# One input tile of a rotary-embedding kernel loaded on ScalarE's DMA ring instead of SyncE's

## The chip, the cores and the metric

One core of one Trainium2 chip. The profile's names for the engines are used: DVE is VectorE, ACT is ScalarE, POOL is GpSimd, PE is TensorE and SP is SyncE. SP and ACT issue the transfers here; the queue of transfers that one of them has issued is called its ring. A transfer moves as packets and has landed when its completion is signalled. The metric is the device time of one execution in microseconds (us), measured over several executions. The profile's span is about 1.8 us shorter than this time. Each timed kernel was run in rounds beside the kernel before on the same chip.

## The reference

```python
# x: 8 x 8 x 1024 x 64 float32; cos, sin: 1024 x 32 float32
x_first, x_second = x[..., :32], x[..., 32:]
out_first  = x_first * cos - x_second * sin
out_second = x_first * sin + x_second * cos
return concatenate([out_first, out_second], axis=-1)
```

x has 16.8 MB and so has the output. There are four multiplications and two additions for each pair of elements, so that most of the work is moving bytes.

## The kernel before

x is cut into 16 tiles of 128 partitions x 2048 elements (1.05 MB, 8 KB per partition). All 16 fit in SBUF at once and every tile has its own place, so no load waits for a buffer. The two tables come first, one on each ring; then all of x on SP's ring:

```python
nc.sync.dma_start(out=sn[0:Q], in_=sin_cached...)      # SP's ring
nc.scalar.dma_start(out=cs[0:Q], in_=cos_cached...)    # ACT's ring

xt = []
for first, n in [(0, 1), (1, 1)] + [(c, 2) for c in range(2, n_ch, 2)]:
    t = xp.tile([P, n, F], fp32, name=f"x{first}")
    nc.sync.dma_start(out=t, in_=xf[first:first + n]...)
    xt += [t[:, i] for i in range(n)]
```

The tables arrive on 32 partitions. DVE copies sine and ACT copies cosine into PSUM on all 128 partitions; POOL copies both within SBUF for its own tiles. Then the tiles are shared out:

```python
def vector_pool(c, cuts=(0, R)):      # DVE: products, POOL: sums, store on SP's ring
    s = tv.tile([P, F], fp32, name="vs")
    products(nc.vector, c, s, csp, snp)
    for n0, n1 in zip(cuts, cuts[1:]):
        sums(nc.gpsimd, c, s, n0, n1)
        store(nc.sync, c, n0, n1)
# vector_tensor(c): products on DVE, sums by TensorE, copied back by ACT, store on ACT's ring
# on_pool(c): all on POOL, store on SP's ring
def vector_alone(c):                  # all on DVE, store on ACT's ring
    products(nc.vector, c, acc, csp, snp)
    sums(nc.vector, c, acc, 0, R)
    store(nc.scalar, c)

vector_tensor(0)
on_pool(1)
vector_pool(2)
# ... (cut: 3 to 13)
vector_pool(14, (0, G, R))
vector_alone(15)
```

Tile 0 is DVE's first work on x. Tile 1, the one that the change moves, is POOL's first.

Of the kernel before, what the change touches and what calls it, by code (L numbers as in the profile page):

```python
# [1 line left out]

# [4 lines left out]


@with_exitstack
def kernel(  # L10
    ctx: ExitStack,
    tc: tile.TileContext,
    x: bass.AP,
    cos_cached: bass.AP,
    sin_cached: bass.AP,
    out: bass.AP,
):
    nc = tc.nc
    fp32 = mybir.dt.float32
    TT = mybir.AluOpType  # L20
    P = nc.NUM_PARTITIONS

    b, h, seq, hd = x.shape
    half = hd // 2
    R = 32
    F = R * hd
    T = R * half
    Q = seq // R
    reps = P // Q
    n_ch = (b * h * seq) // (R * P)  # L30
    G = 512 // half
    assert seq % R == 0 and P % Q == 0 and Q % 32 == 0

    xf = x.rearrange("b h s d -> (b h s d)").rearrange(
        "(c p m) -> c p m", p=P, m=F)
    of = out.rearrange("b h s d -> (b h s d)").rearrange(
        "(c p m) -> c p m", p=P, m=F)

    ctx.enter_context(tc.manual_schedule())
    const = ctx.enter_context(tc.tile_pool(name="const", bufs=1))  # L40
    xp = ctx.enter_context(tc.tile_pool(name="xp", bufs=1))
    tv = ctx.enter_context(tc.tile_pool(name="tv", bufs=6))
    tg = ctx.enter_context(tc.tile_pool(name="tg", bufs=1))
    pt = ctx.enter_context(
        tc.tile_pool(name="pt", bufs=1, space=bass.MemoryType.PSUM))
    pa = ctx.enter_context(
        tc.tile_pool(name="pa", bufs=1, space=bass.MemoryType.PSUM))

    cs = const.tile([P, T], fp32, name="cs")
    sn = const.tile([P, T], fp32, name="sn")  # L50
    plus = const.tile([P, P], fp32, name="plus")
    minus = const.tile([P, P], fp32, name="minus")
    csp = pt.tile([P, T], fp32, name="csp")
    snp = pt.tile([P, T], fp32, name="snp")
    acc = pa.tile([P, F], fp32, name="acc")


    nc.sync.dma_start(out=sn[0:Q], in_=sin_cached.rearrange("(p n) j -> p (n j)", p=Q))
    nc.scalar.dma_start(out=cs[0:Q], in_=cos_cached.rearrange("(p n) j -> p (n j)", p=Q))


    xt = []
    for first, n in [(0, 1), (1, 1)] + [(c, 2) for c in range(2, n_ch, 2)]:
        t = xp.tile([P, n, F], fp32, name=f"x{first}")
        nc.sync.dma_start(out=t, in_=xf[first:first + n].rearrange("c p m -> p c m"))
        xt += [t[:, i] for i in range(n)]

    nc.gpsimd.memset(plus, 0.0)
    nc.gpsimd.affine_select(out=plus, in_=plus, compare_op=TT.not_equal, fill=1.0,
                            base=0, pattern=[[-1, P]], channel_multiplier=1)  # L70
    nc.scalar.mul(minus, plus, -1.0)  # L71
    for r in range(reps):
        nc.vector.tensor_copy(out=snp[r * Q:(r + 1) * Q], in_=sn[0:Q])  # L73
        nc.scalar.copy(out=csp[r * Q:(r + 1) * Q], in_=cs[0:Q])  # L74
    for t in (sn, cs):
        for r in range(1, reps):
            nc.gpsimd.tensor_copy(out=t[r * Q:(r + 1) * Q], in_=t[0:Q])  # L77

    def rows(t, n0=0, n1=R):
        return t[:, n0 * hd:n1 * hd].rearrange("p (n k j) -> p n k j", k=2, j=half)  # L80

    def tab(t, n0=0, n1=R):
        v = t[:, n0 * half:n1 * half].rearrange("p (n o j) -> p n o j", o=1, j=half)
        return v.to_broadcast([P, n1 - n0, 2, half])

    def products(eng, c, s, ctab, stab):
        xr = rows(xt[c])
        eng.tensor_tensor(out=rows(s), in0=xr, in1=tab(stab), op=TT.mult)  # L88
        eng.tensor_tensor(out=xr, in0=xr, in1=tab(ctab), op=TT.mult)  # L89

    def sums(eng, c, s, n0, n1):
        xr, sr = rows(xt[c], n0, n1), rows(s, n0, n1)
        eng.tensor_tensor(out=xr[:, :, 0], in0=xr[:, :, 0], in1=sr[:, :, 1], op=TT.subtract)  # L93
        eng.tensor_tensor(out=xr[:, :, 1], in0=xr[:, :, 1], in1=sr[:, :, 0], op=TT.add)  # L94

    def store(q, c, n0=0, n1=R):
        q.dma_start(out=of[c][:, n0 * hd:n1 * hd], in_=xt[c][:, n0 * hd:n1 * hd])

    def on_pool(c):
        s = tg.tile([P, F], fp32, name="gs")  # L100
        products(nc.gpsimd, c, s, cs, sn)
        sums(nc.gpsimd, c, s, 0, R)
        store(nc.sync, c)

    def vector_pool(c, cuts=(0, R)):
# [6 lines that stand above are left out]
    def vector_tensor(c):  # L112
        s = tv.tile([P, F], fp32, name="vs")
        products(nc.vector, c, s, csp, snp)
        for n0 in range(0, R, G):
            xr, sr = rows(xt[c], n0, n0 + G), rows(s, n0, n0 + G)
            a = acc[:, n0 * hd:(n0 + G) * hd].rearrange("p (k n j) -> p k n j", k=2, j=half)
            for k in range(2):
                nc.tensor.matmul(a[:, k], plus, xr[:, :, k], start=True, stop=False)  # L119
                nc.tensor.matmul(a[:, k], plus if k else minus, sr[:, :, 1 - k],  # L120
                                 start=False, stop=True)
            nc.scalar.copy(out=xr, in_=a.rearrange("p k n j -> p n k j"))  # L122
        store(nc.scalar, c)

    def vector_alone(c):
# [7 lines that stand above are left out]
    vector_pool(3)  # L133
    vector_tensor(4)
    on_pool(6)
    vector_pool(5)
    vector_tensor(7)
    vector_pool(8)
    vector_tensor(9)
    vector_pool(10)  # L140
    vector_tensor(11)
    vector_pool(12)
    vector_pool(13)
    vector_pool(14, (0, G, R))
    vector_alone(15)

# [1 line left out]
_INS = ['x', 'cos_cached', 'sin_cached']  # L148
_OUTS = [((8, 8, 1024, 64), 'float32')]


# [23 lines left out]
```

## Time and profile before

| | before |
|---|---|
| time, median of 3 | 85.98 us (85.84 to 86.1) |
| span of the profiled execution | 84.16 us |
| moved by DMA | 33.82 MB |
| tile 0 lands, tile 1 lands, tiles 2 and 3 land | 6.48, 9.03, 13.96 us |
| DVE takes tile 0, POOL takes tile 1 | 8.87, 10.44 us |
| last store issued; its first packet; its landing | 77.22, 79.86, 83.16 us |

Landings, first packets and packet durations in this document are the trace's records of single transfers and packets. The prediction below shows the lines of the profile that carry the reading. The rings' shares are two lines of the page more (packets, MB, share of the time of 16 DMA engines; q1 is SP's ring, q10 ACT's):

```profile
q1 hardware_dynamic: 3824, 27.40, 78.7%
q10 hardware_dynamic: 912, 6.42, 18.1%
```

Together the rings take 97% of all 16 engines' time over the span, start and end included. Both shares are of the same 16 engines' time, so it is this sum that can be full, not a ring of its own.

### The profile page before, as it was taken

How to read it: one execution, taken by the hardware profiler on the slowest of the kernel's cores; microseconds unless marked ns; L12 is line 12 of the kernel's file. 1: busy time of each engine (PE TensorE's matmuls, PEld its weight loads, DVE VectorE, ACT ScalarE, POOL GpSimd, SP SyncE). 2: the span in 40 equal slices, each digit the busy share in tenths (PEclk: the TensorE clock that was granted, in tenths of full speed). 3: DMA queues.
4: the chain of work that ended last, by engine and by line, in shares of the span. 5: the costliest groups of instructions: out<-in, count | busy, mean ns of one | idle time of the engine just before them, and what ended most of it. 6: DMA issues, size and time to landing. Idle time of an engine off the chain costs nothing.

```text
span 84.2 us, 363 instructions
## 1 busy us (share of the span) xinstructions
PE 40.1 (48%) x80; PEld 15.7 (19%) x80; DVE 70.4 (84%) x34; ACT 15.7 (19%) x16; POOL 71.4 (85%) x38
## 2 busy tenths in 40 slices
PE   0000005994930896895949497794949600000000
PEld 0000002422400341423314051332414100000000
DVE  0199997999999999999999982999999999996000
ACT  4399000004040003104040402204040310000000
POOL 3199999999999999999999999999999999970000
PEclk9999999999999569999999999999999999555555
DMA  3899999999999999999999999999999999999991
GB/s 29 282 432 409 420 420 436 417 409 420 436 428 409 417 428 432 432 424 409 421 436 436 432 421 417 424 424 436 432 432 432 413 421 428 428 436 407 432 419 55
DMA packets 4736, 33.82 MB, mean 402 GB/s; under 512 B 448, under 2 KB 448, under 8 KB 768
## 3 DMA queue, kind: packets, MB, share of 16 engines
q1 hardware_dynamic: 3824, 27.40, 78.7%
q10 hardware_dynamic: 912, 6.42, 18.1%
HBM read 17.04 MB, written 16.78 MB: 402 GB/s over the span
## 4 chain that ended last, share of the span: by engine, by line
POOL 53%; DVE 23%; issue 9%; DMA 4%; DVEq 1%; POOLq 0%
POOL x L94 13%; POOL x L93 11%; DVE vs L88 11%; POOL x L89 11%; POOL gs L88 11%; DVE x L89 8%; POOL sn L77 4%; DMA sn<-in_sin_cached_dram 4%; POOL cs L77 3%; DVE acc L88 3%; DVE x L93 1%; DVEq L170 1%; POOLq L93 0%; POOLq L77 0%
## 5 line engine op out<-in xcount | busy, mean ns | idle before, releaser
L119 PE MATMUL acc<-x,plus 128*128 128x512 f32 x40 | 23.3, 666 | 26.4 <-DVE x L89 13.6
L89 DVE TENSOR_TENSOR x<-x,csp 128x2048 f32<-128x2048 f32 x14 | 32.0, 2287 | 0.6
L88 DVE TENSOR_TENSOR vs<-x,snp 128x2048 f32<-128x2048 f32 x13 | 29.7, 2282 | 2.2 <-POOL x L94 1.7
L122 ACT COPY x<-acc 128x1024 f32<-128x1024 f32 x10 | 10.1, 1012 | 49.2 <-PE acc L120 49.2
L94 POOL TENSOR_TENSOR x<-x,vs 128x1024 f32<-128x1024 f32 (+1 forms) x9 | 19.0, 2108 | 0.0
L93 POOL TENSOR_TENSOR x<-x,vs 128x1024 f32<-128x1024 f32 (+1 forms) x9 | 18.9, 2105 | 0.0
L119 PEld LDWEIGHTS acc<-x,plus 128*128 128x128 f32 x40 | 7.5, 208 | 39.4 <-issue 23.9
L120 PE MATMUL acc<-vs,minus 128*128 128x512 f32 x20 | 11.6, 666 | 0.0
L120 PE MATMUL acc<-vs,plus 128*128 128x512 f32 x20 | 10.2, 592 | 0.0
L89 POOL TENSOR_TENSOR x<-x,cs 128x2048 f32<-128x2048 f32 x2 | 9.1, 4546 | 0.2
L88 POOL TENSOR_TENSOR gs<-x,sn 128x2048 f32<-128x2048 f32 x2 | 9.1, 4542 | 0.1
L73 DVE COPY snp<-sn 32x1024 f32<-32x1024 f32 x4 | 4.9, 1223 | 3.9 <-DMA sn<-in_sin_cached_dram 3.8
L120 PEld LDWEIGHTS acc<-vs,minus 128*128 128x128 f32 x20 | 4.4, 219 | 5.9 <-issue 5.9
L77 POOL COPY sn<-sn 32x1024 f32<-32x1024 f32 x3 | 3.1, 1032 | 2.7 <-DMA sn<-in_sin_cached_dram 2.6
L93 POOL TENSOR_TENSOR x<-x,gs 128x1024 f32<-128x1024 f32 x2 | 4.7, 2362 | 0.2
L94 POOL TENSOR_TENSOR x<-x,gs 128x1024 f32<-128x1024 f32 x2 | 4.7, 2357 | 0.0
L120 PEld LDWEIGHTS acc<-vs,plus 128*128 128x128 f32 x20 | 3.8, 190 | 4.8 <-issue 4.8
L74 ACT COPY csp<-cs 32x1024 f32<-32x1024 f32 x4 | 4.0, 1008 | 1.5 <-DMA cs<-in_cos_cached_dram 1.4
L77 POOL COPY cs<-cs 32x1024 f32<-32x1024 f32 x3 | 3.1, 1033 | 0.1
L88 DVE TENSOR_TENSOR acc<-x,snp 128x2048 f32<-128x2048 f32 x1 | 2.3, 2297 | 0.0
L71 ACT ACT_TABLE_LOAD x1 | 1.3, 1283 | 1.2 <-PEq L159 1.2
L93 DVE TENSOR_TENSOR x<-x,acc 128x1024 f32<-128x1024 f32 x1 | 1.2, 1223 | 0.0
(8 smaller groups left out, 2.4 us busy)
## 6 DMA issues: line engine op xcount, KB each, us to landing
x<-in_x_dram SPq DMA_DIRECT2D x7, 2048.0 KB, 25.0
out_dram<-x SPq DMA_DIRECT2D x9, 1024.0 KB, 13.0
out_dram<-x ACTq DMA_DIRECT2D x6, 1024.0 KB, 9.0
x<-in_x_dram SPq DMA_DIRECT2D x2, 1024.0 KB, 6.3
out_dram<-x SPq DMA_DIRECT2D x2, 512.0 KB, 6.0
cs<-in_cos_cached_dram ACTq DMA_DIRECT2D x1, 128.0 KB, 3.4
sn<-in_sin_cached_dram SPq DMA_DIRECT2D x1, 128.0 KB, 3.1
```

The lines of the kernel that those rows point to most:

```text
L71: nc.scalar.mul(minus, plus, -1.0)
L73: nc.vector.tensor_copy(out=snp[r * Q:(r + 1) * Q], in_=sn[0:Q])
L74: nc.scalar.copy(out=csp[r * Q:(r + 1) * Q], in_=cs[0:Q])
L77: nc.gpsimd.tensor_copy(out=t[r * Q:(r + 1) * Q], in_=t[0:Q])
L88: eng.tensor_tensor(out=rows(s), in0=xr, in1=tab(stab), op=TT.mult)
L89: eng.tensor_tensor(out=xr, in0=xr, in1=tab(ctab), op=TT.mult)
L93: eng.tensor_tensor(out=xr[:, :, 0], in0=xr[:, :, 0], in1=sr[:, :, 1], op=TT.subtract)
L94: eng.tensor_tensor(out=xr[:, :, 1], in0=xr[:, :, 1], in1=sr[:, :, 0], op=TT.add)
L119: nc.tensor.matmul(a[:, k], plus, xr[:, :, k], start=True, stop=False)
L120: nc.tensor.matmul(a[:, k], plus if k else minus, sr[:, :, 1 - k], start=False, stop=True)
L122: nc.scalar.copy(out=xr, in_=a.rearrange("p k n j -> p n k j"))
L170: with _tile.TileContext(nc) as tc:
```

## The change

Tile 1 is the first x that POOL needs, and it stands behind tile 0 on SP's ring while ACT's ring is idle after the cosine table. The intent is to let ACT issue it, so that it moves beside tile 0 and SP comes sooner to the later loads.

```diff
     for first, n in [(0, 1), (1, 1)] + [(c, 2) for c in range(2, n_ch, 2)]:
         t = xp.tile([P, n, F], fp32, name=f"x{first}")
-        nc.sync.dma_start(out=t, in_=xf[first:first + n].rearrange("c p m -> p c m"))
+        (nc.scalar if first == 1 else nc.sync).dma_start(
+            out=t, in_=xf[first:first + n].rearrange("c p m -> p c m"))
         xt += [t[:, i] for i in range(n)]
```

## The prediction

> **What bounds the kernel now.** I read four views, in this order: the page's slices and chain, the stretches (busy time and DMA rate by window), the DMA view of short windows, and the timelines of the first 20 us and of the end.
>
> The page first. The tempting reading is the chain of waits: POOL and DVE carry it and DMA has 4%. But the row of DMA slices contradicts it.
>
> ```profile
> DVE  0199997999999999999999982999999999996000
> DMA  3899999999999999999999999999999999999991
> POOL 53%; DVE 23%; issue 9%; DMA 4%; DVEq 1%; POOLq 0%
> ```
>
> DVE and POOL stop three to four slices before the end, while DMA stays at nine tenths from the third slice to the last but one. The stretches give the rates (columns: window, its length, busy us of PE, PEld, DVE, ACT and POOL with instruction counts, granted clock, DMA share, GB/s):
>
> ```profile
> 2.00:3.00 1.00, 0.00 (x0) 0.00 (x0) 0.00 (x0) 0.77 (x2) 0.00 (x0) 1.00 0.63 217
> 3.00:4.00 1.00, 0.00 (x0) 0.00 (x0) 0.16 (x1) 0.00 (x0) 0.05 (x1) 1.00 0.98 279
> 4.00:24.00 20.00, 9.08 (x16) 3.52 (x16) 19.25 (x11) 5.17 (x6) 19.55 (x10) 1.00 1.02 424
> 24.00:48.00 24.00, 16.27 (x32) 6.39 (x32) 23.79 (x12) 4.57 (x5) 23.84 (x10) 0.93 1.01 423
> 48.00:82.00 34.00, 14.80 (x32) 5.75 (x32) 27.21 (x13) 4.41 (x5) 27.27 (x14) 0.85 1.01 427
> ```
>
> From 4 to 82 us the DMA share is 1.01 to 1.02: no engine has a free moment, and the rate is flat whether only loads run (4 to 24), loads and stores (24 to 48) or stores alone. The packet records say why: nearly every packet is 8192 bytes and takes 309 ns, and 16 engines x 8192 B / 309 ns = 424 GB/s. In these 78 us 20 x 424 + 24 x 423 + 34 x 427 = 33.15 thousand GB/s x us, that is 33.15 MB of the 33.82 MB in all. So the time is: about 2.5 us of start, 33.82 MB at about 424 GB/s (79.8 us), and about 2 us for the last receipt and the end of the program: 84.2 us of span. The measured 85.98 us lies 1.8 us above the span, and I carry that difference over unchanged.
>
> Is the end set by the last compute or by the queue of bytes? The last store is issued on ACT at 77.22, when DVE is done. The DMA view of the two windows after it:
>
> ```profile
> q1 hardware_dynamic: 281, 1.02, 100.1%
> ...
> q10 hardware_dynamic: 143, 1.05, 91.9%
> ```
>
> The first line is 77.3 to 79.8 us: SP's ring (q1) alone fills all 16 engines with stores issued earlier. The second is 79.8 to 82.5 us: now ACT's ring (q10) moves the last tile. Its first packet comes 2.64 us after its issue. On nearly empty rings the sine table's first packet came 1.0 us after its issue (0.73 to 1.75), the first x tile's 1.7 us. So the last store could be issued some 0.9 to 1.6 us later (an estimate from these) before the engines ran dry, and issuing it earlier would bring nothing.
>
> **What the Trainium skill says.** The page "DMA: Bandwidth & Descriptors", section "Issuing engines are not separate DMA queues", says that transfers begun by different engines run on the same 16 DMA engines and interleave, and that issuing from several saves only the sequencers' issue time. The trace agrees: 424 GB/s with SP's ring alone, 423 and 427 with both. The same page, section "Queues, rings and completion order", says that each DMA engine takes turns between the rows that have work, packet by packet. The trace agrees: while the first ACT store moved, from 28.5 to 33.1 us, the two rings had
>
> ```profile
> q10 hardware_dynamic: 128, 1.05, 53.8%
> q1 hardware_dynamic: 112, 0.92, 47.1%
> ```
>
> packets in the ratio 128 to 112. Its section "Specifications" puts the fabric's ceiling at 435 GB/s; the 424 to 427 of the trace are 97 to 98% of it, so a second ring has little left to find. Its section "Latency and other measured facts" gives about 0.6 us to the first byte from these issuers; the trace shows 1.0 us at best and 3.6 us for ACT's stores behind a full SP ring (24.91 to 28.51), and I use the trace's.
>
> **The change part by part.**
>
> Bytes: nothing is added or removed. 28 transfers, 33.82 MB, packets of the same size to the same places. At 424 GB/s this is 79.8 us before and after.
>
> Issue time: SP loses one load issue of 0.42 us, so its second load (tiles 2 and 3) is issued near 1.64 rather than 2.11. It sits behind the first tile in a ring whose first x packet moves at 2.9 us and which is never empty: worth nothing. ACT gains one issue of about 0.42 us at 1.18, ahead of its table load (1.28 us) and the negation (0.31 us). These end near 3.2 instead of 2.78. ACT's next work waits for the cosine table at 4.16:
>
> ```profile
> 1.18 1.28 ACT L71 ACT_TABLE_LOAD   x1 [1.18 <-PEq L159]
> 2.47 0.31 ACT L71 ACTIVATE minus<-plus 128x128 f32<-128x128 f32 x1
> 4.16 4.13 ACT L74 COPY csp<-cs 32x1024 f32<-32x1024 f32 x4 [1.38 <-DMA cs<-in_cos_cached_dram]
> ```
>
> So 0.42 of 1.38 us of idle time is used: cost 0. Both tables are ahead of any x data in their rings, so they should land as before (3.81 and 4.13).
>
> Landing of the first tiles: this is the only thing that moves. Before, 128 packets of tile 0 went first, then 128 of tile 1: they landed at 6.48 and 9.03 us, and tiles 2 and 3 at 13.96. Each tile is 8 packets per DMA engine, 8 x 309 ns = 2.47 us. After, the two rings take turns, so that both tiles move from about 2.9 us and both end at about the time when two tiles have moved. I expect tile 0 at 8.0 to 9.0 us, later by 1.5 to 2.5, and tile 1 at 8.5 to 9.5. Tiles 2 and 3 still come after 2 tiles and the tables: 13.9 to 14.1.
>
> Who feels it? DVE and POOL:
>
> ```profile
> 3.84 5.00 DVE L73 COPY snp<-sn 32x1024 f32<-32x1024 f32 x4 [3.84 <-DMA sn<-in_sin_cached_dram]
> 8.87 2.29 DVE L88 TENSOR_TENSOR vs<-x,snp 128x2048 f32<-128x2048 f32 x1
> 11.26 2.29 DVE L89 TENSOR_TENSOR x<-x,csp 128x2048 f32<-128x2048 f32 x1
> 13.99 2.29 DVE L88 TENSOR_TENSOR vs<-x,snp 128x2048 f32<-128x2048 f32 x1 [0.44 <-DMA x<-in_x_dram]
> 7.17 3.18 POOL L77 COPY cs<-cs 32x1024 f32<-32x1024 f32 x3
> 10.44 4.52 POOL L88 TENSOR_TENSOR gs<-x,sn 128x2048 f32<-128x2048 f32 x1
> ```
>
> DVE copies the sine table until 8.84 and only then touches tile 0, so a landing of up to 8.84 is free and one at 9.0 costs 0.2 us. That is swallowed at once by the 0.44 us that DVE waits for tile 2 at 13.99. POOL touches tile 1 at 10.44, about 1 us or more after any landing that I expect. TensorE starts up to 0.2 us later on tile 0, with 3.9 us of idle time ahead of its next tile. Sum on compute: 0 us. On the path that sets the end, the bytes: 0 us, less whatever the start gains (next).
>
> **The rivals.**
>
> *The second ring fills the start better.* From 3 to 4 us the rate is 279 and not 424 GB/s, so 145 KB are missing, or 0.34 us; the first packets of a tile are slow. With two rings holding x data at 2.9 us, part of the gap could close. Against it: the DMA share there is already 0.98, so the packets are slow rather than missing. I give it 0 to 0.2 us, a mean of 0.05: 85.8 to 85.98.
>
> *Tile 0 lands late enough to hold the DVE.* If ACT's ring got more than its turn, or the first packets were slower with two rings, tile 0 could land at 9.5. DVE would then reach tile 2 at about 14.2 instead of 13.99 and POOL, which has its own chain from the sine table, would not see it. A shift of 0.2 to 0.5 us at the end of DVE falls within the 0.9 to 1.6 us of slack of the last store. Time: 86.0 still, at the worst 86.3.
>
> *A new wait on ACT.* A transfer reuses an earlier one's completion semaphore and must wait for that landing; SP's stores do this (one waited 8.1 us for a load). With tile 1 on ACT the assignment may shift, and an ACT store might wait for a late load, which would block ACT's copies from PSUM. ACT has 3.8 to 10.8 us idle before each first copy of a tile, and SP's ring keeps the engines full meanwhile. Only a hold-up of many us would count. I give it 2%: 87 to 89.
>
> *A clear gain*, because tile 1 comes sooner on its own queue: this would need POOL to be waiting for tile 1, and POOL waits for nothing there; it is still copying tables. Under 1%.
>
> **Range and chances.** The time before less 0.05 us for the start gives 85.93; I predict 85.9. The three runs before span 85.84 to 86.1; with that scatter, the 0.2 us that the start might give, and 0.3 for late tiles, the range is 85.5 to 86.35. Faster by over 2% would need under 84.3, which is less than the bytes allow unless the rate itself rose: 1%. Slower by over 2% needs a wait that empties the rings: 2%. Within 2%: 97%.
>
> **What would show each step right or wrong.** Right: DMA share 1.01 or so and 423 to 427 GB/s from 4 to 82 us; ACT's ring up by 1.05 MB (6.42 to about 7.47 MB) and SP's down by the same; tile 0 landing near 8.5 us and tile 1 within 1 us of it; DVE's first product still at about 8.87, its third still released by the load of tiles 2 and 3 at about 14.0; ACT's table copies still at about 4.16; the last packet at about 82.5. Wrong: a row with DMA share under 0.9 between 4 and 80 us; ACT waiting on a semaphore of a load before a store; a landing of the sine table after 4.0 us, from which the whole chain of POOL hangs; tile 0 after 9.4 us.

## The result, and the profile after

The changed kernel took 86.08 us (median of 6, 85.91 to 86.19) against 85.97 us (median of 6) for the kernel before in the same rounds. The ratio is 1.0014, with a 95% interval of 0.9997 to 1.0031. A ratio here is the mean time of one kernel's runs over that of the other's of the same rounds, so not quite the ratio of the medians. Executions over 1.5% slower than the fastest of the same kernel are left out of the means. Two more sets of rounds gave 1.0012 (0.9997 to 1.0026) and 0.9996 (0.9978 to 1.0014). It is the same time.

The page after, in its lines of slices, rings and issues of single tiles (the number after the KB is us from issue to landing):

```profile
DVE  0299899999999999999999974999999999994000
...
DMA  2999999999999999999999999999999999999991
...
q1 hardware_dynamic: 3680, 26.35, 75.7%
q10 hardware_dynamic: 1056, 7.47, 21.1%
...
x<-in_x_dram ACTq DMA_DIRECT2D x1, 1024.0 KB, 8.3
x<-in_x_dram SPq DMA_DIRECT2D x1, 1024.0 KB, 7.7
```

144 packets and 1.05 MB have gone over from q1 to q10, and nothing else has: 26.35 + 7.47 is again 33.82 MB. Tile 0 (on SP) now takes 7.7 us to land instead of 5.3, tile 1 (on ACT) 8.3. In the stretch from 4 to 8 us, while both move, the DMA view of the changed kernel has

```profile
q10 hardware_dynamic: 109, 0.89, 53.3%
q1 hardware_dynamic: 109, 0.80, 47.9%
```

so the rings share the engines nearly evenly (11 of q1's packets are under 512 bytes, hence its smaller 0.80 MB). The stretches of the changed kernel (columns as in the prediction):

```profile
2.00:3.00 1.00, 0.00 (x0) 0.00 (x0) 0.00 (x0) 0.99 (x2) 0.00 (x0) 1.00 1.36 316
3.00:4.00 1.00, 0.00 (x0) 0.00 (x0) 0.32 (x1) 0.26 (x1) 0.21 (x1) 1.00 0.72 262
4.00:24.00 20.00, 9.10 (x16) 3.52 (x16) 19.21 (x11) 5.04 (x5) 19.55 (x10) 1.00 1.01 424
24.00:48.00 24.00, 16.39 (x32) 6.39 (x32) 23.79 (x12) 4.69 (x5) 23.84 (x10) 0.93 1.01 416
48.00:82.00 34.00, 14.80 (x32) 5.75 (x32) 27.10 (x13) 4.42 (x5) 27.03 (x14) 0.85 1.01 427
```

The rate is what it was, except for 416 instead of 423 GB/s in the middle, to which an experiment returns. Who felt the moved landings is in the timeline of the changed kernel, lines numbered one higher than before (start, duration, instruction, and in brackets the idle time before it and what ended it):

```profile
4.00 4.13 ACT L75 COPY csp<-cs 32x1024 f32<-32x1024 f32 x4 [0.74 <-DMA cs<-in_cos_cached_dram]
...
8.98 2.29 DVE L89 TENSOR_TENSOR vs<-x,snp 128x2048 f32<-128x2048 f32 x1 [0.31 <-DMA x<-in_x_dram]
10.29 4.51 POOL L89 TENSOR_TENSOR gs<-x,sn 128x2048 f32<-128x2048 f32 x1
11.37 2.29 DVE L90 TENSOR_TENSOR x<-x,csp 128x2048 f32<-128x2048 f32 x1
...
13.87 2.29 DVE L89 TENSOR_TENSOR vs<-x,snp 128x2048 f32<-128x2048 f32 x1 [0.21 <-DMA x<-in_x_dram]
```

DVE now waits 0.31 us for tile 0 (landed at 8.88). It then waits only 0.21 us for tiles 2 and 3 instead of 0.44, and starts on them at 13.87, before at 13.99. ACT's extra issue is taken from the 1.38 us that it waited for its table; 0.74 us of that is left. POOL takes tile 1 at 10.29 with no wait, 0.8 us after its landing at 9.52.

### The profile page after: what moved, and what is told of

The parts are those of the page before. It is cut to its first block, busy times and chain, and to the rows that moved or that the text cites. A ratio compares the mean times of both kernels' runs of the same rounds, so it can differ in the third digit from the quotient of the medians.

```text
span 84.4 us, 362 instructions
## 1 busy us (share of the span) xinstructions
PE 40.3 (48%) x80; PEld 15.7 (19%) x80; DVE 70.4 (83%) x34; ACT 15.7 (19%) x16; POOL 71.3 (85%) x38
## 2 busy tenths in 40 slices
DMA packets 4736, 33.82 MB, mean 401 GB/s; under 512 B 448, under 2 KB 448, under 8 KB 768
## 3 DMA queue, kind: packets, MB, share of 16 engines
q1 hardware_dynamic: 3680, 26.35, 75.7%
q10 hardware_dynamic: 1056, 7.47, 21.1%
## 4 chain that ended last, share of the span: by engine, by line
POOL 53%; DVE 23%; issue 9%; DMA 3%; DVEq 1%; POOLq 0%
POOL x L95 13%; POOL x L94 11%; DVE vs L89 11%; POOL x L90 11%; POOL gs L89 11%; DVE x L90 8%; POOL cs L78 4%; POOL sn L78 4%; DMA sn<-in_sin_cached_dram 3%; DVE acc L89 3%; DVE x L94 1%; DVEq L171 1%; POOLq L94 0%; POOLq L78 0%
```

## The experiments

The theory under test: the end is set by the bytes, from the moment the DMA engines are full, and the compute chain has slack in front of the last store. The main rival: the chain through POOL and DVE that the page puts first sets the end. A second one: the change costs a little, by making the transfers rougher.

### One store more

```diff
     vector_pool(2)
+    nc.sync.dma_start(out=of[15], in_=xt[2])
     vector_pool(3)
```

> The kernel before with one more store of 1.05 MB: tile 2 is also written to the place of tile 15, which is overwritten later by its right values. No compute engine does more. Theory (bytes set the end): 128 packets more, 8 per DMA engine, 8 x 309 ns = 2.47 us: 88.3 to 88.6 us, ratio 1.027 to 1.030. Rival (the chain through POOL and DVE sets the end and DMA has room): under 0.5 us.

88.54 us, ratio 1.0297 (1.0279 to 1.0314), results correct: 2.55 us more for 2.47 us of packets. DVE ended as before and the last store was issued at 77.07 us, yet the engines were full for longer. In the stretches of this kernel the row that was empty after 82.4 us before now reads

```profile
82.00:84.00 2.00, 0.00 (x0) 0.00 (x0) 0.00 (x0) 0.00 (x0) 0.00 (x0) 0.50 1.02 430
```

with all five compute columns at zero. A chain of compute can't explain this; the bytes can.

### One store fewer

```diff
         for n0, n1 in zip(cuts, cuts[1:]):
             sums(nc.gpsimd, c, s, n0, n1)
-            store(nc.sync, c, n0, n1)
+            if c != 2:
+                store(nc.sync, c, n0, n1)
```

> The kernel before without the store of tile 2 (a wrong result on purpose). 1.05 MB fewer, compute unchanged. Theory: the bytes would end 2.47 us sooner, but the last store is still issued at 77.2 and needs about 1.0 to 1.7 us to its first packet, so only the slack of 0.9 to 1.6 us can be won: 84.3 to 85.2 us. If the slack were without limit: 83.5. Rival (compute chain): 86.0.

The result is wrong on purpose: tile 2 is not written. 83.81 us, ratio 0.9748 (0.9733 to 0.9763), so 2.17 us less. This is more than I expected, and it is not the whole 2.47 us. The stretches show where it stopped:

```profile
76.00:78.00 2.00, 0.00 (x0) 0.00 (x0) 1.12 (x1) 0.00 (x0) 0.00 (x0) 0.50 0.72 293
78.00:80.00 2.00, 0.00 (x0) 0.00 (x0) 0.00 (x0) 0.00 (x0) 0.00 (x0) 0.50 1.08 446
```

The share of 0.72 is a hole: SP's ring ran out of data near 77.9 us, and the last store, issued at 77.16, moved its first packet at 78.00. From issue to first packet it took 0.84 us when nothing was in the way, against 2.64 us in the kernel before. By its first packet, the slack of the last store is therefore 2.64 - 0.84 = 1.8 us, not the 0.9 to 1.6 of the prediction. By its last packet it is 2.0 us: from issue to there it took 5.48 us before (77.22 to 82.70) and 3.51 here (77.16 to 80.67). Before, SP's ring still moved until 80.24 us beside the store's first packets. It is the last packet that counts for the end.

### One and two DVE products more at the end

```diff
     def vector_alone(c):
         products(nc.vector, c, acc, csp, snp)
+        for _ in range(1):    # in the second kernel: range(2)
+            nc.vector.tensor_tensor(out=csp, in0=cs, in1=cs, op=TT.mult)
         sums(nc.vector, c, acc, 0, R)
```

> The kernel before with one more DVE product of 128x1024 (about 1.2 us, like the rows of that shape; its result is not used) ahead of the last tile's sums. Compute and the issue of the last store move by 1.2 us, no byte is added. Theory (SP's ring keeps the engines full until 79.8 us, the last store has 0.9 to 1.6 us of slack): 0 to 0.4 us longer, 85.9 to 86.4. Rival (the compute chain sets the end): 1.2 us longer, 87.2.

> The same with two such products, 2.4 us. Theory: the slack of 0.9 to 1.6 us is used up and the rest shows: 0.8 to 1.5 us longer, 86.8 to 87.5, and a stretch of idle DMA engines appears near 80 us. Rival (compute chain): 2.4 us longer, 88.4.

With one product the last store was issued at 78.71 us, 1.5 us later than before, and the time was 85.99 us, ratio 1.0001 (0.9986 to 1.0015), as expected. The engines stayed full after the issue:

```profile
80.00:82.00 2.00, 0.00 (x0) 0.00 (x0) 0.00 (x0) 0.00 (x0) 0.00 (x0) 0.50 1.03 436
```

With two it was issued at 79.84, 2.6 us later, and the time was 86.57 us, ratio 1.0075 (1.0059 to 1.0091), 0.64 us more and under the 86.8 to 87.5 that I expected. The issue in the timeline and the stretch of the second kernel:

```profile
79.84 0.34 ACTq L97 DMA_DIRECT2D out_dram<-x  x1
```

```profile
80.00:82.00 2.00, 0.00 (x0) 0.00 (x0) 0.00 (x0) 0.00 (x0) 0.00 (x0) 0.50 0.75 311
```

For the same two microseconds the kernel before had a share of 0.96 and 408 GB/s. The first packet came at 80.68, again 0.84 us after the issue, 0.82 us later than in the kernel before, and the last one ended at 83.34, 3.50 us after the issue and 0.64 later than before. So a delay of 1.5 us is free, and of 2.6 us only the part over the slack shows: 2.6 - 2.0 = 0.6 us, by the last packet and in the time alike. The delays and the dropped store give the same slack from both sides. The compute chain would have cost 1.5 and 2.6 us.

### Another load on ACT's ring too

```diff
-        (nc.scalar if first == 1 else nc.sync).dma_start(
+        (nc.scalar if first in (1, 4) else nc.sync).dma_start(
```

> As the changed kernel, and the load of tiles 4 and 5 goes to ACT's ring too. Theory (a landing matters when an engine waits for it): tiles 2 and 3 now share the engines with tiles 4 and 5, landing near 18 instead of 13.9 us. DVE waits about 4 us longer, gets back the 1.7 us that it waits for a buffer later, and ends 2 to 3 us later; less 0.9 to 1.6 us of slack: 86.5 to 88. Rival (the bytes alone set the end, whatever the order): 86.0.

87.38 us, ratio 1.015 (1.0113 to 1.0187), within what I expected. Tiles 2 and 3 landed at 18.86 instead of 13.85 us, tiles 4 and 5 at 19.27, and DVE had to wait (its timeline):

```profile
18.88 2.29 DVE L89 TENSOR_TENSOR vs<-x,snp 128x2048 f32<-128x2048 f32 x1 [5.18 <-DMA x<-in_x_dram]
```

The last store was issued at 80.94 us, 3.72 later than before, and the span of the profiled execution is 86.05 us, 1.89 longer. (It was the slowest of the four; by the ratio they are 1.3 us over before. The two slower ones had a granted clock of 0.88, the two faster ones 0.91; whether that makes the 0.8 us between them is not tested.) Less the slack of 2.0 us, the later issue would make 1.7. But the engines did not run dry at the end: they were full again from 75 us until the last packets. They ran dry earlier, in a hole among the stretches of this kernel,

```profile
72.00:74.00 2.00, 0.82 (x2) 0.00 (x0) 1.31 (x2) 1.01 (x1) 2.00 (x2) 1.00 0.31 131
```

where the kernel before moved 406 GB/s. By the packets it held nearly 1.7 us of empty engines, most of the 1.89. No store was ready because DVE was late: POOL had waited 3.1 us for a product of DVE until 64.26, and after its store at 68.93 the next one was issued only at 73.53. Here the very same kind of edit costs 1.5%. What tells the two apart is not the ring but who waits for the tile that is delayed: for tile 0, DVE is busy with its table until 8.7 us and gives the rest back at 13.9; for tiles 2 and 3 it stands idle for 5 us. The rival that order never matters is refuted: the bytes set the end only as long as there is something ready to move.

### Tile 1 ahead of the cosine table

```diff
-    nc.scalar.dma_start(out=cs[0:Q], in_=cos_cached...)
     ...
         (nc.scalar if first == 1 else nc.sync).dma_start(
             out=t, in_=xf[first:first + n].rearrange("c p m -> p c m"))
         xt += [t[:, i] for i in range(n)]
+        if first == 1:
+            nc.scalar.dma_start(out=cs[0:Q], in_=cos_cached...)
```

> As the changed kernel, but tile 1 is ahead of the cosine table on ACT's ring. Theory: the place behind the table is what made the change harmless. Here the table waits for 8 packets of tile 1 per DMA engine, taken in turn with tile 0's: it lands near 8.5 to 9.5 us instead of 4.0. POOL's copies of it start then instead of at 7.0, DVE's second product waits for ACT's four copies (4.1 us, so until about 13.3 instead of 11.4). POOL and DVE end about 2 to 2.5 us later; the last store has 0.9 to 1.6 us of slack, so the time is 86.6 to 87.6 us. Rival (order on a ring does not matter, only bytes do): 86.0.

86.18 us (median of 4, 85.92 to 86.76), ratio 1.0035 (1.0004 to 1.0066): my expectation of 86.6 to 87.6 was wrong. The table landed at 7.88 us rather than 8.5 to 9.5, because the rings did not take turns. In the DMA view of this kernel from 2.5 to 5 us:

```profile
q10 hardware_dynamic: 122, 1.00, 100.7%
q1 hardware_dynamic: 17, 0.00, 0.8%
```

Tile 1, issued at 0.73, moved almost alone; tile 0, issued on SP at 1.17, had its first packet at 5.15. POOL waited 1.0 us for the table,

```profile
7.93 3.19 POOL L79 COPY cs<-cs 32x1024 f32<-32x1024 f32 x3 [1.03 <-DMA cs<-in_cos_cached_dram]
```

and the last store was issued at 77.92, 0.7 us later than before. That lies well within the slack of 2.0 us, and by the profile the last store landed at 83.07, before at 83.16. So even this order costs next to nothing. The place behind the table is not what made the change harmless; the slack alone would have covered it. The 0.35% of the ratio I can't place: the profiled execution, the fastest of the four, doesn't show it.

### Both tables on ACT's ring

```diff
-    nc.sync.dma_start(out=sn[0:Q], in_=sin_cached...)
+    nc.scalar.dma_start(out=sn[0:Q], in_=sin_cached...)
     nc.scalar.dma_start(out=cs[0:Q], in_=cos_cached...)
```

> The kernel before with both tables on ACT's ring, so that tile 0 is first on SP's. Theory (what counts besides bytes is when the engines are first full of x data): tile 0's first packet moves at 1.8 to 2.0 instead of 2.9 us; the tables land up to 0.4 us later, and with them the compute chain, within the slack. 0.3 to 0.8 us shorter: 85.2 to 85.7. Rival (the tables' landing sets the end through POOL's chain): 0.2 to 0.5 us longer, 86.2 to 86.5.

86.89 us, ratio 1.0115 (1.0088 to 1.0142): slower, where the theory had it 0.3 to 0.8 us faster. Tile 0's first packet did move at 1.74 us, as expected. But the sine table landed at 4.82 and the cosine table at 8.29, and the last store was issued at 78.38, 1.2 us later. That alone would be within the slack, so the rival is not confirmed either; and SP's ring still filled the engines when the last store came up (first packet at 80.49, 2.1 us after its issue). The missing time lies in the start. Up to 3 us this kernel had moved 213 KB and the kernel before 279, so the earlier first packet of x brought no bytes. From 4 us on it fell behind. One stretch of this kernel and then of the kernel before:

```profile
6.00:8.00 2.00, 0.00 (x0) 0.00 (x0) 1.93 (x3) 0.00 (x0) 1.94 (x2) 1.00 1.04 297
```

```profile
6.00:8.00 2.00, 0.00 (x0) 0.00 (x0) 1.93 (x3) 1.94 (x3) 1.92 (x3) 1.00 0.96 401
```

While the cosine table's packets of 4096 bytes moved between x packets, the DMA engines were booked in full and yet moved only 297 GB/s: from 5.5 to 8.0 us the x packets took 421 ns in the median instead of 314 in the kernel before. Up to 8 us this kernel moved 1.92 MB and the kernel before 2.24 MB; the 0.32 MB between them take 0.75 us at 424 GB/s, and the spans differ by 0.78 us. So the rule of bytes holds, but my step from "x first" to "full sooner" was wrong: nothing was gained before 3 us, and time was lost with the tables in between. Why packets of x are slower beside those of a table is left open.

### Does the change cost a tenth of a microsecond?

In the first profile of the changed kernel 22 of the 8192-byte packets between 26 and 31 us took over 500 ns, in the kernel before none. This is the 416 instead of 423 GB/s. So I ran the changed kernel three times more and the kernel before twice more, once as its own control.

> The changed kernel once more, with five rounds and a second profile. In its first profile the DMA rate fell to 303 GB/s in one of the 40 slices (near 27 to 29 us) and the loads after it landed 0.5 us later; DVE ended 0.2 us earlier than before. Theory (the bytes set the end, and the dip is an accident of that one execution): ratio to before 0.998 to 1.003, no dip in the same place. Rival (two rings with x data cost something real): the dip comes again in the same slice and the ratio is 1.002 or more, with an interval clear of 1.

> The kernel before, unchanged, timed against itself. So far the changed kernel has given ratios of 1.0014 and 1.0012 in two sets, and both of its profiles show 19 to 22 slow packets (over 500 ns instead of 309) near 28 us; of five profiles with the order of loads of before one (two products more) shows 20 such packets and four show none to two. If this scatter belongs to the chip and not to the change: ratio 0.9985 to 1.0015, and such a dip in some profile of this order. If it belongs to the change: ratio within 0.0005 of 1 and no dip here.

> One more profile of the kernel before, for the count of slow packets near 28 us. If the change makes them: none. If they come and go: some 16 to 20 in one of this and the control's.

> The changed kernel a third time, on the same chip as the control. If the change really costs 0.1 us: ratio 1.001 to 1.002 again, slow packets near 28 us again. If not: ratio 0.999 to 1.001, and a profile without them can come.

> One more profile of the changed kernel. If the change makes the slow packets near 28 us: 16 to 22 again, so four in four. If they come and go: one of this and the third is free of them.

| | ratio to before (95%) | slow packets, 26 to 31 us |
|---|---|---|
| changed, first set | 1.0014 (0.9997 to 1.0031) | 22 |
| changed again | 1.0012 (0.9997 to 1.0026) | 19 |
| changed, third set | 0.9996 (0.9978 to 1.0014) | 9 |
| changed, one look (86.04 us, state unknown) | | 3 |
| before, first profile | | 0 |
| before, its own control | 0.9985 (0.9969 to 1.0002) | 1 |
| before, one look (86.12 us, state unknown) | | 10 |
| before with two products more | | 20 |

The slow stretch in the changed kernel and in the kernel before with two products more, whose loads are those of before:

```profile
27.00:30.00 3.00, 2.37 (x3) 1.17 (x4) 2.96 (x3) 0.00 (x0) 3.00 (x2) 0.58 1.00 341
```

```profile
27.00:30.00 3.00, 2.41 (x5) 1.21 (x6) 2.96 (x3) 0.00 (x0) 3.00 (x2) 0.83 0.98 344
```

The kernel before had 426 GB/s there in its first profile, 388 in its control's and 363 in its single look. The dip comes with the old order of loads too and can be nearly absent with the new one, so the change is not needed for it. The excess of the 22 packets over 309 ns, spread over 16 engines, is 0.38 us, of the order of what the spans with the dip are longer by (84.4 against 84.15 us). Whether the change makes it somewhat more frequent, four profiles against seven with the old loads (0, 0, 1, 1, 2, 10 and 20) can't settle; the two other kernels with tile 1 on ACT's ring had 2 and 3. An unchanged kernel against itself gave 0.9985, so these rounds can't tell a ratio of 1.0014 from 1.

## Why the prediction was right

**The bound.** It rested on the bytes and not on the chain of waits that the page puts first. The extra store (2.55 us for 2.47 us of packets), the dropped store (2.17 us less) and the free delay of 1.5 us on DVE show it from three sides. One reading was loose: packets of 8192 bytes are 96% of the bytes, but 3968 of 4736 packets.

**The bytes of the change.** 7.47 MB on ACT's ring was predicted and came; the rate from 4 to 24 us stayed at 424 GB/s. From 24 to 48 us it was 416, under the 423 to 427 that the prediction named as a sign of being right; that is the dip above, which the prediction did not foresee.

**The landings.** Tile 0 at 8.88 (predicted 8.0 to 9.0), tile 1 at 9.52 (8.5 to 9.5, so just over the edge), tiles 2 and 3 at 13.85 (13.9 to 14.1, so just under). The rings did take turns here.

**Who waits.** DVE's first product moved by 0.11 us and its wait for tiles 2 and 3 took that back, as worked out. POOL didn't wait. ACT's work before the table was later by 0.48 us (predicted 0.42), and 0.74 of its 1.38 us of idle time was left; the rest went because its table landed 0.15 us sooner. The sine table landed at 3.60 to 3.82 us in the four profiles of the changed kernel and at 3.69 to 3.96 in the seven with the old loads; the last store was issued up to 0.2 us sooner for it, which brought nothing, as the slack says.

**The start.** I gave the second ring 0 to 0.2 us. In the first profiles the changed kernel had moved 35 x 2 + 316 + 262 = 648 KB up to 4 us, the kernel before 558. But this is within the scatter: the seven profiles with the old loads had moved 557 to 656 KB by then, the four of the changed kernel 533 to 655. A gain at the start is not shown, and none reached the end: the three sets give a time that is the same or a tenth of a microsecond longer. So the 0.05 us by which I put the time under the one before was no insight, and this term of the sum could have been left at zero.

**The slack.** I put it at 0.9 to 1.6 us, from latencies of 1.0 and 1.7 us at the start of the program. By the same reckoning it is 1.8 us, as the latency of a store with rings run dry is 0.84 us; by the last packet it is 2.0. The mis-sizing was on the safe side, and two of my later expectations missed by it: the dropped store gained more and the two products cost less. With tile 1 ahead of the table the miss was another: I had the end of the compute 2 to 2.5 us later, and it was 0.7.

**The new wait on ACT.** It did not come: no ACT store in the changed kernel waited for a load.

## What to carry to other kernels

Read whether the DMA engines are full before you read the chain of waits: where the rate is flat at its ceiling from start to end, moving a transfer to another ring adds no rate; it changes the order of landings. Then ask of each landing that comes later who waits for it and how much of that wait is given back at the next one: 2.4 us later for tile 0 cost nothing, 5 us later for tiles 2 and 3 cost 1.5%. To find the slack of the compute in front of a full queue, add a known delay in two sizes and watch for the hole; it is cheaper and surer than estimating latencies.

## What the Trainium skill lacked or had wrong

- "DMA: Bandwidth & Descriptors", section "Latency and other measured facts", gives about 0.6 us to the first byte. The runs show 0.84 us from the start of the issue (0.5 us from its end; the page doesn't say where it starts to count) to the first packet of a store with the rings run dry (twice), 1.0 us for the first table, 2.64 us for the last store behind SP's ring, and 3.6 us for an earlier store on ACT's ring beside a full one on SP's. In the last two the wait behind another ring's transfers is the larger part, and it is not in that figure.
- The same page, section "Queues, rings and completion order", has each engine take turns between the rings that have work. With tiles 0 and 1 issued within 0.01 us of each other the rings did (109 and 109 packets, 0.89 and 0.80 MB, from 4 to 8 us). With tile 1 issued 0.44 us ahead on the other ring they did not: 122 packets to 17 of 0.00 MB from 2.5 to 5 us. Whether the earlier issue or the table's later place decided this is not tested.
- No page that I read has the case seen here, in which the DMA engines' busy share is full at a low rate: 1.04 at 297 GB/s, with x packets at 421 instead of 314 ns, while a table of 4096-byte packets on 32 partitions moved between them.
- No page that I read has the stretch of 0 to 22 slow packets (over 500 ns) near 28 us, worth up to 0.4 us, that comes and goes between profiles.
